# Splitting three of ten weight tiles with two GpSimd-queue loads instead of ScalarE and VectorE

## The chip, the cores and the metric

The kernel runs on one core of one Trainium2 chip. The metric is device time in microseconds (us) of one execution; a timed comparison gives the median of several runs of each kernel on the same chip. Engines are named as the profile names them: PE (TensorE matmul), PEld (TensorE weight load), DVE (VectorE), ACT (ScalarE), POOL (GpSimd), SP (SyncE, which here issues the loads).

## The reference

Two transformer-like blocks are run one after the other on 256 tokens of width 2048, all in float32. The first has a two-way gated recurrence, a short convolution, an output projection and a gated feed-forward; the second has a long convolution, an attention with forget gates, an attention over 256 memory rows and an output projection. The change touches the first block's feed-forward alone:

```python
D_FF = -(-8 * D_MODEL // (3 * 256)) * 256          # 5632
...
h2 = _rmsnorm(x, ffn_norm_w[l])
g, u = jnp.split(jnp.einsum('bsd,df->bsf', h2, w_gate_up[l]), 2, axis=-1)
x = x + jnp.einsum('bsf,fd->bsd', jax.nn.silu(g) * u, w_down[l])
```

## The kernel before, in words

*Products from parts.* TensorE multiplies float32 through the type F32R. To keep the precision, each operand is split in a high part (the value copied to F32R) and a low part (the value minus the high part), and a product is three matmuls: high x high, high x low, low x high (`tri`, lines 645 to 647; `proj`, lines 166 to 168). The activations are split once and kept in "units" (tiles of `upool`, eight buffers). The weights stream: `split` (L131) is `load` (L113: SP brings 256 rows x 512 columns, 512 KB, into a tile `raw`) followed by `parts_of` (L120: ACT copies `raw` to `wh`, then DVE subtracts `wl = raw - wh`). Since the helpers `act` (L63) and `tt` (L54) record every operation, ACT and DVE work stands under those two lines in the profile and is told apart by its tiles.

*Rings.* `raw_tile` (L108) takes the load tiles in turn: four of pool `wraw` outside the feed-forward, and during it `wraw` and `wraw2` (four each) alternately, so eight. The pairs `wh`, `wl` come from `wsp` (four) and, in the feed-forward, `wsx` (two), in a turn of six. A load can be issued only when the tile that it takes has been read for the last time.

*The feed-forward.* The 5632 hidden columns are worked in 11 pieces of 512 (index f). `hidden_pre(f)` (L649) computes gate and up products of one piece over eight steps p of 256 input rows each. In steps 0, 1, 3, 5, 7 the gate tile and the up tile are each split and multiplied plainly: two tiles of 12 products of 512 columns each, ten tiles a piece. In steps 2, 4, 6 a seven-product scheme is used (L685 to L711): DVE forms combinations `Ta` and `Tb` of the two loaded tiles, which are split too, and TensorE does 21 products. After p = 5 the bank X4 is read out and the hidden tile of the piece before is transposed there (`turn`, L733, line 739). At the end DVE and ACT combine the banks to the hidden tile `hd` (L713 to L730). All eight PSUM banks (five of `pmm`, three of `phd`) serve one piece.

*Parts.* The pieces are grouped in three parts (0 to 3, 4 to 7, 8 to 10; L748). After each part the down projection (`proj` with `w_down`, four column blocks) adds what its pieces contribute to the residual tile X (`residual`, two DVE additions a column block). The four units that hold the input of the feed-forward live through the whole stage; the units of a part's hidden tiles live until its down projection has read them.

*Order of the work.* The program is written in the order of the data; a scheduler with a timeline of its own orders the instructions on each engine, and `high_priority` (4000 for the splits) moves work ahead as far as its buffers allow. On each engine and queue the order is then fixed, and an instruction that waits holds those behind it.

Of the kernel before, what the change touches and what calls it, by code (L numbers as in the profile page):

```python
# [8 lines left out]
F32 = mybir.dt.float32  # L9
F32R = mybir.dt.float32r  # L10
# [3 lines left out]
ALU = mybir.AluOpType  # L14
# [6 lines left out]
CW = 512  # L21
# [8 lines left out]
def tile_two_blocks(  # L30
# [4 lines left out]
    nc = tc.nc  # L35
    x, mem, out = x[0], mem_2[0], out[0]
    w_in, w_out, w_gate_up, w_down = w_in[0], w_out[0], w_gate_up[0], w_down[0]
# [4 lines left out]
    wraw = ctx.enter_context(tc.tile_pool(name="wraw", bufs=4))  # L42
# [7 lines left out]
    def stt(out, in0, scalar, in1, op0, op1):  # L50
        nc.vector.scalar_tensor_tensor(out=out, in0=in0, scalar=scalar, in1=in1, op0=op0, op1=op1)  # L51

    def tt(out, a, b, op):
        nc.vector.tensor_tensor(out=out, in0=a, in1=b, op=op)  # L54
# [7 lines left out]
    def act(out, in_, func=AF.Copy, **kw):  # L62
        nc.scalar.activation(out=out, in_=in_, func=func, **kw)  # L63
# [4 lines left out]
    def bank(shape):  # L68
        return phd.tile(shape, F32, tag="h", name="h")
# [5 lines left out]
    def new_unit():  # L75
        return upool.tile([128, 4, 2, T], F32R, tag="u", name="u")
# [28 lines left out]
    more_raw = []  # L105
    more_w = []

    def raw_tile(nk, n):  # L108
        raw = (more_raw[-1] if more_raw else wraw).tile([128, nk, n], F32, tag="raw", name="raw")
        more_raw.reverse()  # L110
        return raw

    def load(w, r0, nk, c0, n):  # L113
        raw = raw_tile(nk, n)
        nc.sync.dma_start(
            out=raw, in_=w[r0:r0 + nk * 128, c0:c0 + n].rearrange("(k p) n -> p k n", p=128)
        )
        return raw

    def parts_of(raw, pool=None):  # L120
        if pool is None:
            pool = more_w[0] if more_w else wsp
            if more_w:
                more_w.append(more_w.pop(0))
        wh = pool.tile(list(raw.shape), F32R, tag="wh", name="wh")
        wl = pool.tile(list(raw.shape), F32R, tag="wl", name="wl")
        act(wh, raw)
        tt(wl, raw, wh.bitcast(F32), ALU.subtract)
        return wh, wl

    def split(w, r0, nk, c0, n, pool=None):  # L131
        with tc.high_priority(4000):
            return parts_of(load(w, r0, nk, c0, n), pool)

    def mm_bank():
        return pmm.tile([128, CW], F32, tag="p", name="p")
# [9 lines left out]
    def two(a):  # L146
        return a.rearrange("p (h b) -> p h b", h=2)
# [195 lines left out]
    with tc.tile_pool(name="rows", bufs=1) as rows:  # L343
        vb = rows.tile([nv, 128], F32, name="vb")
        for name, src, n in vectors:
            nc.gpsimd.dma_start(
                out=vb[off[name]:off[name] + n], in_=src.rearrange("(a b) -> a b", b=128)
# [26 lines left out]
    with tc.tile_pool(name="mk", bufs=1) as mkp:  # L374
# [11 lines left out]
        out=cums[:, :128], in_=cums[:, :128], pattern=[[1, 128]], compare_op=ALU.is_ge, fill=0.0,  # L386
# [5 lines left out]
        out=cmask, in_=cmask, pattern=[[-1, 128]], compare_op=ALU.is_ge, fill=NEG,  # L392
# [158 lines left out]
    for hf in range(2):  # L551
# [5 lines left out]
        for j in range(2):  # L557
# [4 lines left out]
            for a in range(2):  # L562
                k = 2 * j + a
                w = [cw3[:, 8 * i + 4 * hf + k:8 * i + 4 * hf + k + 1] for i in range(3)]
# [35 lines left out]
    ff = ExitStack()  # L600
    fp = ff.enter_context(tc.tile_pool(name="fp", bufs=1))
# [33 lines left out]

    more_raw.extend([wraw, ff.enter_context(tc.tile_pool(name="wraw2", bufs=4))])
    wsx = ff.enter_context(tc.tile_pool(name="wsx", bufs=2))
    more_w.extend([wsp, wsp, wsx, wsp, wsp, wsx])  # L640

    def tri(pt, left, right, st, sp):
        (xh, xl), (wh, wl) = left, right
        mh, ml = in_turn(wh), in_turn(wl)
        nc.tensor.matmul(pt, lhsT=xh, rhs=mh, start=st, stop=False)  # L645
        nc.tensor.matmul(pt, lhsT=xh, rhs=ml, start=False, stop=False)  # L646
        nc.tensor.matmul(pt, lhsT=xl, rhs=mh, start=False, stop=sp)  # L647

    def hidden_pre(f, between):  # L649

        five, three = [mm_bank() for i in range(5)], [bank([128, CW]) for i in range(3)]
        if f % 2:
            P2, P1, P4, P3, X4 = five
            P6, P7, P5 = three
        else:
            P1, P2, P6, P7, P5 = five
            P3, P4, X4 = three
        begun = set()

        def prod(pt, left, right, end=False):  # L660
            tri(pt, left, right, id(pt) not in begun, end)
            begun.add(id(pt))

        for p in range(8):
            u, a0 = x1u[p // 2], 2 * (p % 2)
            r0, end = 256 * p, p == 7

            def x_(a, t):
                sl = slice(t * 128, (t + 1) * 128)
                return u[:, a0 + a, 0, sl], u[:, a0 + a, 1, sl]  # L670

            if p not in sums7:
                for (b0, b1), c0 in (((P2, P4), f * CW), ((P3, X4), DFF + f * CW)):
                    wh, wl = split(w_gate_up, r0, 2, c0, CW)
                    for a in range(2):
                        for t, b in enumerate((b0, b1)):
                            prod(b, x_(a, t), (wh[:, a], wl[:, a]), a == 1 and (end or (b is X4 and p == 5)))
                if p == 5:
                    x4 = fp.tile([128, CW], F32, tag="x4", name="x4")
                    with tc.high_priority(4000):  # L680
                        act(x4, X4)
                    between(X4)
                    begun.discard(id(X4))
                continue
            F = sums7[p]  # L685
            with tc.high_priority(4000):
                g_ = load(w_gate_up, r0, 2, f * CW, CW)
                u_ = load(w_gate_up, r0, 2, DFF + f * CW, CW)
                B1 = parts_of(g_)
                Ta, Tb = (fp.tile([128, 2, CW], F32, tag=n, name=n) for n in ("Ta", "Tb"))  # L690
                tt(Ta[:, 0], u_[:, 0], g_[:, 0], ALU.subtract)
                tt(Ta[:, 1], u_[:, 1], u_[:, 0], ALU.subtract)
                W13 = parts_of(Ta)
                tt(Tb[:, 0], u_[:, 1], Ta[:, 0], ALU.subtract)
                tt(Tb[:, 1], g_[:, 1], Tb[:, 0], ALU.subtract)
                W24 = parts_of(Tb)
                B22 = parts_of(u_[:, 1:2])

            def at(w, a):
                return w[0][:, a], w[1][:, a]  # L700

            def form(i):
                return F[:, i, 0], F[:, i, 1]

            prod(P1, x_(0, 0), at(B1, 0), p == 6)
            prod(P2, x_(1, 0), at(B1, 1))
            prod(P5, form(0), at(W13, 0), p == 6)
            prod(P7, form(2), at(W13, 1), p == 6)
            prod(P6, form(1), at(W24, 0), p == 6)
            prod(P4, x_(1, 1), at(W24, 1))  # L710
            prod(P3, form(3), at(B22, 0))  # L711

        u2 = fp.tile([128, CW], F32, tag="u2", name="u2")  # L713
        u3 = fp.tile([128, CW], F32, tag="u3", name="u3")
        g = fp.tile([128, NT, CW], F32, tag="g", name="g")
        h = fp.tile([128, NT, CW], F32, tag="hd", name="hd")
        with tc.high_priority(4000):
            act(g[:, 0], P1)
            tt(u2, P6, g[:, 0], ALU.add)
            tt(u3, P7, u2, ALU.add)  # L720
            tt(g[:, 0], P2, g[:, 0], ALU.add)
            tt(x4, x4, u3, ALU.add)
            tt(g[:, 1], P4, u3, ALU.add)
            tt(x4, P5, x4, ALU.add)
            tt(u2, P5, u2, ALU.add)
            tt(x4, X4, x4, ALU.add)
            tt(u2, P3, u2, ALU.add)
        for t, up_ in enumerate((u2, x4)):
            act(g[:, t], g[:, t], AF.Silu, scale=rs1[:, t:t + 1])
            stt(two(h[:, t]), ordered(up_), rs1[:, t:t + 1], ordered(g[:, t]), ALU.mult, ALU.mult)  # L730
        return h
# [13 lines left out]

    st = new_stats()
    x2u = []
    for part in (range(0, 4), range(4, 8), range(8, 11)):  # L748
        gu = []
        waiting = lambda ps: None  # L750
        for f in part:
            h = hidden_pre(f, waiting)
            gu.append((new_unit(), f * CW))
            waiting = turn(h, gu[-1][0])
        waiting(bank([128, CW]))
        for c in range(4):
            residual(proj(gu, w_down, c * CW), c)
            if part[-1] == 10:
                x2u.append(unit_from(xk(c), lambda k, c=c: wfg[:, 4 * c + k:4 * c + k + 1]))
                stats_piece(st, xc(c), c)  # L760
# [290 lines left out]
    for u, r0 in out_units:  # L1051
        for k0 in (0, 2):
            pool = lw if len(parts) < 6 else wsp
            parts.append((u, k0, split(w_out2, r0 + k0 * 128, 2, 3 * CW, CW, pool)))
    for t in range(NT):
        sl = slice(t * 128, (t + 1) * 128)
        n = CW if t == 0 else CW // 2
        for c0 in range(0, CW, n):
            pt = mm_bank()[:, :n]
            cs = slice(c0, c0 + n)  # L1060
            for i, (u, k0, (wh, wl)) in enumerate(parts):
                for a in range(2):
                    k = k0 + a
# [7 lines left out]
            part = small.tile([128, 1], F32, tag="part", name="part")  # L1071
# [50 lines left out]
```

## Time and profile before

| | |
|---|---|
| three runs, median | 1612.77 us (1611.62 to 1613.57) |
| profiled execution | 1613.91 us |
| its span | 1611.9 us |
| mean granted TensorE clock | 0.998 |
| feed-forward stage, first to last start of L645 and after (in the span) | 523.4 to about 1166 us |
| loads from `w_gate_up` | 176 of 512.0 KB, 4.6 us in the median from issue to landing |

The profile describes one execution by its span; the execution's own time is longer by what lies around the span. A line of groups names line, engine, operation, tiles, count, busy time and mean, and behind the last bar the idle time of the engine just before them with what ended it. A row of waits names who waited for whom, the sum in us, how often, and the longest. A row of windows gives the busy time of each engine in a stretch with the number of instructions, then the granted clock, the DMA engines' busy share and GB/s. A row of the chain gives start, duration and what. A row of the DMA list gives count, size and the median time from issue to landing.

### The profile page before, as it was taken

How to read it: one execution, taken by the hardware profiler on the slowest of the kernel's cores; microseconds unless marked ns; L12 is line 12 of the kernel's file. 1: busy time of each engine (PE TensorE's matmuls, PEld its weight loads, DVE VectorE, ACT ScalarE, POOL GpSimd, SP SyncE). 2: the span in 40 equal slices, each digit the busy share in tenths (PEclk: the TensorE clock that was granted, in tenths of full speed). 3: DMA queues.
4: the chain of work that ended last, by engine and by line, in shares of the span. 5: the costliest groups of instructions: out<-in, count | busy, mean ns of one | idle time of the engine just before them, and what ended most of it. 6: DMA issues, size and time to landing. Idle time of an engine off the chain costs nothing.

```text
span 1611.9 us, 22433 instructions
## 1 busy us (share of the span) xinstructions
PE 1591.7 (99%) x8433; PEld 1411.7 (88%) x8433; DVE 1245.7 (77%) x1726; ACT 886.4 (55%) x1156; POOL 23.1 (1%) x57
## 2 busy tenths in 40 slices
PE   8999999999999999999999999999999999999998
PEld 7999999999988888888888888888889889998987
DVE  7769768765667899976699975799877999766754
ACT  4657557554545665543565554455546545555643
POOL 3000000000000000000000000000000000000000
PEclk9999999999999999999999999999999999999999
DMA  8765566466686666676666676666756567656564
GB/s 291 215 193 167 145 178 189 144 184 209 203 303 213 184 199 205 202 238 201 193 205 197 184 243 207 182 197 201 243 155 205 148 197 221 183 157 197 164 216 141
DMA packets 166892, 318.36 MB, mean 198 GB/s; under 512 B 12248, under 2 KB 13168, under 8 KB 166784
## 3 DMA queue, kind: packets, MB, share of 16 engines
q1 hardware_dynamic: 164304, 312.19, 62.8%
q10 hardware_dynamic: 2032, 4.60, 0.8%
q8 instruction: 66, 1.08, 0.3%
q14 instruction: 42, 0.34, 0.1%
q0 software_dynamic: 448, 0.14, 0.1%
HBM read 313.74 MB, written 3.15 MB: 197 GB/s over the span
## 4 chain that ended last, share of the span: by engine, by line
PE 77%; DVE 16%; issue 4%; DMA 3%; ACT 1%; ACTq 0%; DVEq 0%; POOLq 0%; POOL 0%
PE p L194 18%; PE p L167 11%; PE p L168 11%; PE p L166 11%; PE p L195 9%; DVE wl L54 8%; DMA raw<-in_w_gate_up_dram 2%; PE h L446 2%; PE p L646 2%; PE p L647 2%; PE p L645 2%; DVE Tb L54 1%; PE h L646 1%; PE h L647 1%; PE h L645 1%
## 5 line engine op out<-in xcount | busy, mean ns | idle before, releaser
L54 DVE TENSOR_TENSOR wl<-raw,wh 128x1024 fp32r<-128x1024 f32 (+1 forms) x580 | 685.0, 1193 | 269.0 <-ACT wh L63 265.8
L63 ACT ACTIVATE wh<-raw 128x1024 fp32r<-128x1024 f32 (+1 forms) x580 | 589.6, 1029 | 516.5 <-PE p L168 169.8
L194 PE MATMUL p<-u,wh 128*128 128x512 f32 x1392 | 458.7, 383 | 0.6 <-DVE sg L54 0.6
L195 PE MATMUL p<-u,wl 128*128 128x256 f32 x1392 | 365.6, 274 | 0.9 <-DVE wl L54 0.8
L167 PE MATMUL p<-wl,u 128*128 128x512 f32 x832 | 318.0, 383 | 0.9 <-DVE wl L54 0.9
L166 PE MATMUL p<-wh,u 128*128 128x512 f32 x832 | 313.3, 381 | 1.7 <-ACT u L63 1.2
L168 PE MATMUL p<-wh,u 128*128 128x512 f32 x832 | 313.6, 382 | 0.7 <-DVE u L51 0.7
L194 PEld LDWEIGHTS p<-u,wh 128*128 128x128 f32 x1392 | 260.1, 190 | 31.3 <-DVE sg L54 1.1
L195 PEld LDWEIGHTS p<-u,wl 128*128 128x128 f32 x1392 | 266.5, 191 | 8.3 <-DVE wl L54 1.6
L166 PEld LDWEIGHTS p<-wh,u 128*128 128x128 f32 x832 | 157.2, 189 | 24.1 <-ACT u L63 2.0
L167 PEld LDWEIGHTS p<-wl,u 128*128 128x128 f32 x832 | 157.5, 189 | 22.7 <-DVE wl L54 1.3
L168 PEld LDWEIGHTS p<-wh,u 128*128 128x128 f32 x832 | 157.0, 190 | 22.1 <-DVE u L51 1.3
L646 PE MATMUL p<-wl,u 128*128 128x512 f32 x341 | 130.1, 383 | 2.3 <-DVE wl L54 2.3
L647 PE MATMUL p<-wh,u 128*128 128x512 f32 x341 | 128.3, 379 | 0.0
L645 PE MATMUL p<-wh,u 128*128 128x512 f32 x341 | 123.7, 380 | 0.0
L646 PE MATMUL h<-wl,u 128*128 128x512 f32 x198 | 75.4, 381 | 2.0 <-DVE wl L54 2.0
L646 PEld LDWEIGHTS p<-wl,u 128*128 128x128 f32 x341 | 64.4, 189 | 14.3 <-DVE wl L54 5.6
L647 PE MATMUL h<-wh,u 128*128 128x512 f32 x198 | 75.1, 379 | 0.0
L645 PE MATMUL h<-wh,u 128*128 128x512 f32 x198 | 74.6, 382 | 0.3 <-DVE u L54 0.2
L645 PEld LDWEIGHTS p<-wh,u 128*128 128x128 f32 x341 | 64.5, 189 | 9.0
L647 PEld LDWEIGHTS p<-wh,u 128*128 128x128 f32 x341 | 64.5, 189 | 8.7
L54 DVE TENSOR_TENSOR Ta<-raw 128x512 f32<-128x512 f32 x66 | 42.8, 694 | 29.7 <-DMA raw<-in_w_gate_up_dram 29.5
(313 smaller groups left out, 1705.4 us busy)
## 6 DMA issues: line engine op xcount, KB each, us to landing
raw<-in_w_in_dram SPq DMA_DIRECT2D x232, 512.0 KB, 4.0
raw<-in_w_gate_up_dram SPq DMA_DIRECT2D x176, 512.0 KB, 4.6
raw<-in_w_down_dram SPq DMA_DIRECT2D x88, 512.0 KB, 4.9
raw<-in_w_out_dram SPq DMA_DIRECT2D x64, 512.0 KB, 4.8
raw<-in_w_mem_kv_dram SPq DMA_DIRECT2D x14, 512.0 KB, 6.1
xp<-in_x_dram SPq DMA_DIRECT2D x4, 512.0 KB, 7.1
X<-in_x_dram SPq DMA_DIRECT2D x4, 512.0 KB, 7.3
mp<-in_mem_dram SPq DMA_DIRECT2D x3, 512.0 KB, 7.6
```

The lines of the kernel that those rows point to most:

```text
L54: nc.vector.tensor_tensor(out=out, in0=a, in1=b, op=op)
L63: nc.scalar.activation(out=out, in_=in_, func=func, **kw)
L166: nc.tensor.matmul(pt[t], lhsT=u[:, k, 0, sl], rhs=mh, start=st, stop=False)
L167: nc.tensor.matmul(pt[t], lhsT=u[:, k, 0, sl], rhs=ml, start=False, stop=False)
L168: nc.tensor.matmul(pt[t], lhsT=u[:, k, 1, sl], rhs=mh, start=False, stop=sp)
L194: nc.tensor.matmul(pt[f], lhsT=wh[:, a, fs], rhs=both, start=st, stop=False)
L195: nc.tensor.matmul(pt[f][:, :T], lhsT=wl[:, a, fs], rhs=high, start=False, stop=False)
L446: nc.tensor.matmul(ps[:, h], lhsT=k[:, h, s * 128:(s + 1) * 128], rhs=q[:, h, t * 128:(t + 1) * 128], start=True, stop=True,)
L645: nc.tensor.matmul(pt, lhsT=xh, rhs=mh, start=st, stop=False)
L646: nc.tensor.matmul(pt, lhsT=xh, rhs=ml, start=False, stop=False)
L647: nc.tensor.matmul(pt, lhsT=xl, rhs=mh, start=False, stop=sp)
```

## The change

For p = 1, 3 and 5 the gate tile is no longer loaded and split by SP, ACT and DVE. A tile of 2048 columns takes both parts. A load on the GpSimd queue with a change of type writes the high part straight from the weights; ACT writes its negative to the low part; a second GpSimd-queue load adds the same weights to the low part. For p = 1 and 5 the tile is a new one, `fl`, with one buffer; for p = 3 it is a unit of `upool`. The load tiles become six (`wraw` four, `wraw2` two, in the turn wraw, wraw, wraw2). The pieces are grouped in four parts: 0 to 2, 3 to 5, 6 to 8, 9 and 10.

```diff
     def raw_tile(nk, n):
-        raw = (more_raw[-1] if more_raw else wraw).tile([128, nk, n], F32, tag="raw", name="raw")
-        more_raw.reverse()
-        return raw
+        pool = more_raw[0] if more_raw else wraw
+        if more_raw:
+            more_raw.append(more_raw.pop(0))
+        return pool.tile([128, nk, n], F32, tag="raw", name="raw")
...
+    def split_in_flight(pair, w, r0, c0):
+
+        wh, wl = pair
+        src = w[r0:r0 + 256, c0:c0 + CW].rearrange("(k p) n -> p k n", p=128)
+        with tc.high_priority(6000):
+            nc.gpsimd.dma_start(out=wh, in_=src)
+            act(wl, wh.bitcast(F32), scale=-1.0)
+            nc.gpsimd.dma_start(out=wl, in_=src, accum_op=ALU.add)
+        return wh, wl
...
-    more_raw.extend([wraw, ff.enter_context(tc.tile_pool(name="wraw2", bufs=4))])
+    wraw2 = ff.enter_context(tc.tile_pool(name="wraw2", bufs=2))
+    more_raw.extend([wraw, wraw, wraw2, wraw, wraw, wraw2])
...
-                    wh, wl = split(w_gate_up, r0, 2, c0, CW)
+                    if p in (1, 3, 5) and b0 is P2:
+                        if p == 3:
+                            unit = new_unit().rearrange("p a b t -> p (a b t)")
+                        else:
+                            unit = fp.tile([128, 2048], F32R, tag="fl", name="fl")
+                        halves_ = (unit[:, i * 1024:(i + 1) * 1024] for i in range(2))
+                        pair = [x.rearrange("p (k n) -> p k n", k=2) for x in halves_]
+                        wh, wl = split_in_flight(pair, w_gate_up, r0, c0)
+                    else:
+                        wh, wl = split(w_gate_up, r0, 2, c0, CW)
...
-    for part in (range(0, 4), range(4, 8), range(8, 11)):
+    for part in (range(0, 3), range(3, 6), range(6, 9), range(9, 11)):
```

## The prediction, made before the changed kernel was built

> **What bounds the kernel now.** I read the page first, then busy time by stage, then the waits of the gated feed-forward stage, then its chain.
>
> ```profile
> span 1611.9 us, 22433 instructions
> PE 1591.7 (99%) x8433; PEld 1411.7 (88%) x8433; DVE 1245.7 (77%) x1726; ACT 886.4 (55%) x1156; POOL 23.1 (1%) x57
> PE 77%; DVE 16%; issue 4%; DMA 3%; ACT 1%; ACTq 0%; DVEq 0%; POOLq 0%; POOL 0%
> ```
>
> TensorE is the bound, but 16% of the chain lies on VectorE. The change touches only the feed-forward stage (523 to 1166 us). By stretches, one gate-up piece (one f) each, except 698:773, which is a down projection, and 1141:1166, the last part's turn to it:
>
> ```profile
> core 0: us, PE busy (x) PEld busy (x) DVE busy (x) ACT busy (x) POOL busy (x), PEclk, DMA share, GB/s
> 698.00:773.00 75.00, 75.00 (x353) 65.66 (x352) 45.47 (x45) 32.23 (x32) 0.00 (x0) 1.00 0.70 213
> 814.50:856.00 41.50, 41.50 (x193) 35.65 (x192) 37.91 (x46) 23.12 (x26) 0.00 (x0) 1.00 0.64 204
> 856.00:897.50 41.50, 39.84 (x186) 33.84 (x185) 37.91 (x47) 24.16 (x28) 0.00 (x0) 1.00 0.61 190
> 1062.00:1103.00 41.00, 41.00 (x194) 35.91 (x193) 37.45 (x46) 23.18 (x27) 0.00 (x0) 1.00 0.64 204
> 1141.00:1166.00 25.00, 25.00 (x124) 21.84 (x122) 19.65 (x22) 11.72 (x13) 0.00 (x0) 1.00 0.77 239
> ```
>
> DVE is busy 37.9 of 41.5 us in a gate-up piece and 45.5 of 75 in a down projection; ACT has 17 us to spare per piece, POOL all of it. What TensorE can do at best comes from its starts: two rows of the timeline in an unbroken run of 33 products, and four transposes before the next product.
>
> ```profile
> 689.52 0.60 PE L739 MATMUL p<-ident,hd 128*128 128x128 f32 x4
> 689.87 0.46 PE L168 MATMUL p<-wh,u 128*128 128x512 f32 x1
> 690.17 0.38 PE L166 MATMUL p<-wh,u 128*128 128x512 f32 x1
> 697.29 0.38 PE L646 MATMUL p<-wl,u 128*128 128x512 f32 x1
> ```
>
> 7.12 us / 33 = 0.216 us a product, whatever the 0.38 us written beside it. A piece has five plain p of 24 products and three seven-product p of 21, so 183, and 8 transposes at 0.35/4: 183 x 0.216 + 0.7 = 40.2 us. The chain shows what it takes once it has fallen behind, and the groups of VectorE in that piece show why:
>
> ```profile
> 842.23 4.58 DMA raw<-in_w_gate_up_dram
> 850.56 1.14 DVE wl L54
> 855.17 1.13 DVE wl L54
> 883.77 4.54 DMA raw<-in_w_gate_up_dram
> 892.07 1.14 DVE wl L54
> L54 DVE TENSOR_TENSOR wl<-raw,wh 128x1024 fp32r<-128x1024 f32 x13 | 15.9, 1233 | 0.0
> L54 DVE TENSOR_TENSOR Ta<-raw 128x512 f32<-128x512 f32 x6 | 3.9, 704 | 3.6 <-DMA raw<-in_w_gate_up_dram 3.6
> ```
>
> The same subtraction stands at 850.56 and 892.07: 41.5 us a piece, 1.3 over TensorE's 40.2. DVE's loop fills them: 37.9 of work and one 3.6 us wait at Ta for a load that could be issued only when a load tile came free. Over the stage, TensorE's loss is
>
> ```profile
> DVE Ta L54 <- DMA raw<-in_w_gate_up_dram: 27.7, 10, 3.6
> PEld p L646 <- DVE wl L54: 5.6, 10, 1.2
> PEld h L646 <- DVE wl L54: 3.7, 5, 1.2
> PEld h L645 <- DVE u L54: 1.8, 4, 0.6
> ```
>
> 5.6 + 3.7 = **9.3 us** of weight loads held up by wl (the 1.8 us for u is the turned hidden tile, which the change leaves). This is all that there is to win here: 0.6%.
>
> **The change part by part.** Of the ten plain tiles of each piece three (p = 1, 3, 5, gate half) lose their SP load, ACT copy and DVE subtraction. A POOL cast load writes wh, ACT writes minus wh to wl, a POOL adding load puts the weights on top. Over 11 pieces: 33 SP loads and 33 subtractions go, 66 POOL loads come, ACT keeps its count.
>
> *DVE.* 3 x 1.13 = 3.4 us less a piece: 41.5 - 3.4 = 38.1, under TensorE's 40.2 with the Ta wait still in it. So the wl waits go: **-9.3**. Of the 1.3 us a piece only the part beyond TensorE's pace was ever lost, so more is not to be had; I keep **+1.0** for waits that come from the order of DVE's work, not its sum. What is late next is ACT (23 to 24 us a piece) and then nothing.
>
> *Four parts for three.* One more turn to a down projection and four more pairs of residual additions (8 x 0.69 = 5.5 us of DVE, by the Ta rows' size; beside 29.5 us of its idle time in a down projection: nothing on the path). No wait of lines 166 to 168 stands in the rows after the turns: +0.3. The last part has two pieces, so while the last hidden tile is finished only one unit's 24 products per column block are ready, 5.2 us less cover a block; the next block's products can stand in (five banks). Between 0 and 5.2 I take +1.0, as 1141:1166 shows TensorE full in that place. Shorter parts also give DVE its pause sooner; that is inside the 9.3.
>
> *Six load tiles for eight.* A piece now issues 13 SP loads, so the ring spans 6/13 of a piece (18.6 us) where it spanned 8/16 (20.1). In order, the tile of p = 2's second half now waits for p = 7's first instead of p = 6's, but four to five subtractions then lie before Ta. I take 0; the other end is a second 3.6 us wait, 38.1 + 3.6 = 41.7, 1.5 over TensorE, for the five pieces that are third or later: 6 to 8 us.
>
> *The chain of the two POOL loads* decides. One tile, fl, serves p = 1 and p = 5. Its next cast can start only when TensorE has read it. From the end of p = 1's gate products to p = 5: 12 + 21 + 24 + 21 = 78 products, **16.8 us**; from p = 5's to the next p = 1: 12 + 21 + 24 + 24 = 81 and 8 transposes, **18.2 us**. (p = 3 has a unit of its own and a whole piece.) In that time: cast, negation, addition. The trace has no such load of this size, so by the nearest rows:
>
> ```profile
> raw<-in_w_gate_up_dram SPq DMA_DIRECT2D x176, 512.0 KB, 4.6
> mp<-in_mem_dram SPq DMA_DIRECT2D x1, 128.0 KB, 2.8
> mp<-in_mem_dram ACTq DMA_DIRECT2D x1, 128.0 KB, 4.7
> vm<-in_mem_norm_g_dram ACTq DMA_DIRECT2D x1, 8.0 KB, 2.2
> vb<-in_mem_norm_g_dram POOLq DMA_DIRECT2D x1, 8.0 KB, 4.9
> vb<-in_lb_bwd_dram POOLq DMA_DIRECT2D x1, 4.0 KB, 6.2
> v<-in_conv_w_dram POOLq DMA_DIRECT2D x1, 62.0 KB, 5.2
> L63 ACT ACTIVATE wh<-raw 128x1024 fp32r<-128x1024 f32 x13 | 13.3, 1054 | 5.5 <-PE h L647 3.7 <-PE p L647 1.8
> 10.42 0.54 POOL L352 DMA_DIRECT2D v<-in_conv_w_dram  x1
> ```
>
> Low end: both as SP's, 4.6 + 1.05 + 4.6 = 10.3. High end: POOL's surcharge 6.2 - 2.2 = 4.0 on each, and the addition moves its 512 KB twice (another 4.6 - 2.2 = 2.4): 8.6 + 1.05 + 1.5 behind other ACT work + 11.0 = 22.2. In the crowded start two like 128 KB loads already differ by 1.9, so of POOL's 2.7 (4.9 - 2.2) I count about 1.7: cast 6.3, negation 1.05 + 0.5, addition 6.3 + 1.2 = 7.5, in all **15.4**. It fits by 1.4 us; loads spread, so I put +1.5 for the pieces where it doesn't. The six issues a piece, 6 x 0.54 = 3.2 us, lie on an idle POOL; behind a waiting addition stands only the next cast, whose tile is still being read. ACT waits in order at each negation, wh copies behind it, for two or three us at most if it comes early; it has 17 us a piece.
>
> By the Trainium skill (DMA: Bandwidth & Descriptors, section Anatomy of one DMA) a load issued from GpSimd takes about 2.0 us and its bytes at 436 GB/s, an estimate of 3.2 us here, with which the chain would be 3.2 + 1.6 + 3.2 = 8.0 and the +1.5 would drop out: 1605.8. The trace's 4.9 us for 8 KB says the fixed part is longer in the start of this kernel.
>
> *Sum:* -9.3 + 1.0 + 0.3 + 1.0 + 0 + 1.5 = -5.5. The profiled execution took 1613.9 us (its span and 2.0 around it), 1.1 over the median 1612.8 of the three runs; against the median that is **1607.3**. A change under 0.2% (3.2 us) can't be told from none.
>
> **The rivals.** (a) *Slower: the two loads don't fit.* With a chain of C us each p = 5 waits C - 16.8 (11 times) and each p = 1 within a part C - 18.2 (7 times). The other terms give -7.0, so it breaks even at C = 17.4 and is slower by more than 0.2% from 17.7. At 19: 24 + 6 - 7 = +23, 1636. At 22.2: 59 + 28 - 7 = +80, 1693. For it: one buffer, two loads in series, an addition nobody has timed here; against it: SP's loads land in 4.6 and the order of products can be arranged around a late pair. (b) *No change.* C between 16.9 and 17.7, or the second Ta wait of 6 to 8 us, or the last turn's 5.2: each gives the 9.3 back, 1610 to 1615. (c) *The transfers become the bound.* DMA share is 0.61 to 0.64 in a piece with 16 loads; 13 + 3 casts + 3 additions at double weight make 22, 0.88. From an addition costing 3.0 loads' worth the share passes 1 by (16 + 9)/16 x 0.64; at 4 it is 1.12, 45 us a piece, +53: about 1660. The Trainium skill (the same page, section Issuing engines are not separate DMA queues) speaks for it: loads of all queues run on the same 16 engines, so POOL's queue adds no bandwidth. No run here shows POOL loads beside a full SP stream.
>
> **How the numbers follow.** Forecast, gain kept: 0.52 (1603 to 1609.5 as its own range; 1603.5 is all 9.3 won). No change: 0.18. Two loads too slow: 0.24. Transfers: 0.06. So faster 0.52, same 0.18, slower 0.30. The range starts a little below 1603.5 and reaches into (a) as far as a chain of 19: 1602 to 1636.
>
> **What would show it.** Right: PEld waits on wl in the stage fall from 9.3 to about 1 us, DVE is busy about 34.5 us a piece, and the bare starts of pieces lie 40 to 40.6 apart. The chain: fl's cast lands about 6.3 after issue, its addition about 7.5. Wrong: TensorE waits at L645 or L646 for a DMA or an ACT write of fl (rival a), SP's 4.6 us grows past 7 with a DMA share near 1 (c), or a DVE wait at Ta above 3.6 (b).

## The result, and the profile after

The changed kernel is slower: 1627.62 us in the median of four runs (1625.04 to 1630.81) beside 1613.17 for the kernel before, a ratio of 1.0094 [1.0080, 1.0108], so 0.8 to 1.1% where 0.3% of gain was forecast. The time lies inside the range given, on the wrong side of no change. The profiled execution took 1630.81 us, 3.2 over its median, so the rows below overstate the loss by about a sixth. A run more than 1.5% above the fastest of its kernel counts as slow and stays out of medians and ratios; that is one run below, of the kernel with the negation on GpSimd.

In the new kernel `tri`'s products are L657 to L659, `proj`'s L177 to L179, the casting load is L137, the adding load L139. From the page: the span, the engines, the chain's shares by engine, and the two queues that carry weights (q1 is SP's, q0 GpSimd's; packets, MB, share of 16 engines' span).

```profile
span 1629.1 us, 22469 instructions
PE 1596.4 (98%) x8433; PEld 1413.2 (87%) x8433; DVE 1212.4 (74%) x1701; ACT 880.0 (54%) x1156; POOL 86.9 (5%) x123
PE 74%; DMA 9%; DVE 7%; issue 7%; ACT 2%; POOL 0%; ACTq 0%; POOLq 0%; DVEq 0%
q1 hardware_dynamic: 155328, 294.88, 57.1%
q0 software_dynamic: 18400, 34.75, 10.3%
```

The feed-forward stage as one stretch, from its first product to the first product of the next block, of the kernel before and then of the changed one:

```profile
core 0: us, PE busy (x) PEld busy (x) DVE busy (x) ACT busy (x) POOL busy (x), PEclk, DMA share, GB/s
523.00:1208.00 685.00, 680.00 (x3192) 590.19 (x3191) 565.23 (x660) 369.12 (x415) 1.36 (x4) 1.00 0.65 202
```

```profile
523.00:1225.00 702.00, 685.92 (x3190) 592.12 (x3189) 536.25 (x640) 363.76 (x415) 62.74 (x66) 1.00 0.76 220
```

The whole loss lies here: 702 us for 685, with what follows equally long in both (403 to 404 us). VectorE was relieved as planned, by 565.2 - 536.3 = 29.0 us. What became of it stands in the changed kernel's waits in the stage (who, for whom, us, times, longest):

```profile
DVE wl L54 <- ACT wh L63: 97.0, 66, 6.2
DVE Ta L54 <- DMA raw<-in_w_gate_up_dram: 57.1, 11, 7.9
ACT fl L63 <- DMA fl<-in_w_gate_up_dram: 33.4, 18, 8.8
PEld p L658 <- DVE wl L54: 6.8, 7, 1.9
PEld h L657 <- ACT wh L63: 6.1, 4, 3.0
PEld p L657 <- ACT wh L63: 3.9, 2, 3.5
PEld p L658 <- DMA fl<-in_w_gate_up_dram: 0.4, 1, 0.4
```

VectorE's wait at Ta grew to 57.1 us from 29.5 in the kernel before (27.7 of them after 523 us), by about as much as VectorE was relieved. TensorE waited for the pair `fl` itself only 0.4 us; it waits, as before, for VectorE's wl, and now 10.0 us for ScalarE's wh, where that was 0.8. The page's DMA list (KB each, median us from issue to landing):

```profile
raw<-in_w_gate_up_dram SPq DMA_DIRECT2D x143, 512.0 KB, 4.9
fl<-in_w_gate_up_dram POOLq DMA_DIRECT2D x44, 512.0 KB, 5.9
u<-in_w_gate_up_dram POOLq DMA_DIRECT2D x22, 512.0 KB, 8.4
```

One loss can be followed from end to end in the chain (start, duration, what; fl is p = 5's and p = 1's tile, u here p = 3's):

```profile
597.27 7.47 DMA fl<-in_w_gate_up_dram
...
604.83 1.07 ACT fl L63
...
606.18 1.19 POOL fl L139
607.37 0.76 POOL u L137
608.13 8.88 issue
...
617.06 0.72 POOL u L139
617.77 9.23 DMA fl<-in_w_gate_up_dram
...
628.07 1.05 ACT wh L63
```

GpSimd's queue works through cast, add, cast, add in order. At 608 to 617 it stands at the adding load for u, whose negation sits on ScalarE behind an operation that waits 4.9 us for VectorE; the cast for fl is queued behind it, is issued at 617.77 and takes 9.23 us; ScalarE waits 8.77 us in order for its negation, with wh copies behind. VectorE's wl then waits 6.18 us for wh, and TensorE stops for 2.7 us, until 629.16. In the kernel before, the same stretch of the chain was VectorE at work and the loads that it waits for at Ta.

From 610 to 625 us the DMA engines were full: three loads of SP, then the adding load for u and the cast for fl beside them (columns as above; a share of about 1 means that the times of the packets fill all 16 engines):

```profile
614.00:617.00 3.00, 3.00 (x17) 2.63 (x17) 3.00 (x6) 1.95 (x3) 0.00 (x0) 1.00 1.05 391
619.00:621.00 2.00, 1.96 (x9) 1.61 (x9) 2.00 (x5) 0.00 (x0) 0.00 (x0) 1.00 1.09 242
```

Then comes a cost of its own, in four windows of 1 us of the changed kernel (columns as above):

```profile
628.00:629.00 1.00, 0.00 (x0) 0.00 (x0) 0.00 (x0) 1.00 (x2) 0.54 (x1) 1.00 0.00 0
629.00:630.00 1.00, 0.84 (x3) 0.49 (x3) 0.86 (x1) 1.00 (x3) 0.66 (x1) 1.00 0.00 0
631.00:632.00 1.00, 1.00 (x4) 0.82 (x3) 1.00 (x2) 1.00 (x3) 0.00 (x0) 0.50 0.94 145
634.00:635.00 1.00, 1.00 (x7) 0.87 (x6) 1.00 (x2) 0.00 (x0) 0.00 (x0) 1.00 0.94 360
```

And its products, from the timeline:

```profile
631.40 0.63 PE L659 MATMUL h<-wh,u 128*128 128x512 f32 x1
631.83 0.63 PE L657 MATMUL h<-u 128*128 128x512 f32 x1
632.26 0.63 PE L658 MATMUL h<-u 128*128 128x512 f32 x1
```

After the stop the granted clock is 0.50 for 3.4 us, and products start 0.43 us apart in place of 0.216. This happens twice in the stage (630.3 and 1009.2) and never in this stage of the kernel before. Note also the DMA share of 0.00 from 628 to 630: while all wait, the engines that move data have nothing to do, though they were full until 625.

### The profile page after: what moved, and what is told of

It reads as the page before. It is cut to its first block, busy times and chain, and to the rows that moved or that the text cites. A ratio compares the mean times of both kernels' runs of the same rounds, so it can differ in the third digit from the quotient of the medians.

```text
span 1629.1 us, 22469 instructions
## 1 busy us (share of the span) xinstructions
PE 1596.4 (98%) x8433; PEld 1413.2 (87%) x8433; DVE 1212.4 (74%) x1701; ACT 880.0 (54%) x1156; POOL 86.9 (5%) x123
## 3 DMA queue, kind: packets, MB, share of 16 engines
q1 hardware_dynamic: 155328, 294.88, 57.1%
q0 software_dynamic: 18400, 34.75, 10.3%
## 4 chain that ended last, share of the span: by engine, by line
PE 74%; DMA 9%; DVE 7%; issue 7%; ACT 2%; POOL 0%; ACTq 0%; POOLq 0%; DVEq 0%
PE p L205 18%; PE p L178 10%; PE p L179 9%; PE p L177 9%; PE p L206 9%; DMA fl<-in_w_gate_up_dram 6%; DVE wl L54 3%; PE p L658 2%; PE p L659 2%; PE p L657 2%; PE h L457 2%; DMA raw<-in_w_gate_up_dram 2%; PE h L657 2%; PE h L659 1%; PE h L658 1%
## 5 line engine op out<-in xcount | busy, mean ns | idle before, releaser
L54 DVE TENSOR_TENSOR wl<-raw,wh 128x1024 fp32r<-128x1024 f32 (+1 forms) x547 | 642.0, 1185 | 273.6 <-ACT wh L63 271.7
L63 ACT ACTIVATE wh<-raw 128x1024 fp32r<-128x1024 f32 (+1 forms) x547 | 552.8, 1025 | 461.9 <-PE p L179 138.9
L178 PE MATMUL p<-wl,u 128*128 128x512 f32 x832 | 317.7, 383 | 3.6 <-DVE wl L54 3.5
L177 PE MATMUL p<-wh,u 128*128 128x512 f32 x832 | 311.3, 382 | 2.6 <-DVE g L54 1.7
L179 PE MATMUL p<-wh,u 128*128 128x512 f32 x832 | 311.1, 382 | 2.0 <-DVE u L51 2.0
L178 PEld LDWEIGHTS p<-wl,u 128*128 128x128 f32 x832 | 157.3, 189 | 27.4 <-DVE wl L54 6.6
L177 PEld LDWEIGHTS p<-wh,u 128*128 128x128 f32 x832 | 157.1, 189 | 25.7 <-DVE g L54 2.1
L179 PEld LDWEIGHTS p<-wh,u 128*128 128x128 f32 x832 | 156.5, 189 | 23.2 <-DVE u L51 2.8
L658 PE MATMUL p<-wl,u 128*128 128x512 f32 x245 | 94.1, 384 | 4.2 <-DVE wl L54 4.2
L657 PE MATMUL p<-wh,u 128*128 128x512 f32 x245 | 92.7, 380 | 3.1 <-ACT wh L63 3.1
L659 PE MATMUL p<-wh,u 128*128 128x512 f32 x245 | 92.8, 379 | 0.0
L54 DVE TENSOR_TENSOR Ta<-raw 128x512 f32<-128x512 f32 x66 | 42.4, 682 | 57.2 <-DMA raw<-in_w_gate_up_dram 57.1
L657 PE MATMUL h<-wh,u 128*128 128x512 f32 x162 | 62.8, 391 | 4.6 <-ACT wh L63 4.5
L658 PE MATMUL h<-wl,u 128*128 128x512 f32 x162 | 62.0, 383 | 0.4 <-DVE wl L54 0.4
L659 PE MATMUL h<-wh,u 128*128 128x512 f32 x162 | 61.9, 382 | 0.0
L658 PEld LDWEIGHTS p<-wl,u 128*128 128x128 f32 x245 | 46.3, 189 | 12.8 <-DVE wl L54 6.7
L657 PEld LDWEIGHTS p<-wh,u 128*128 128x128 f32 x245 | 46.3, 189 | 10.5 <-ACT wh L63 3.5
L659 PEld LDWEIGHTS p<-wh,u 128*128 128x128 f32 x245 | 46.4, 189 | 6.2
```

Source lines behind the costliest of these rows:

```text
L177: nc.tensor.matmul(pt[t], lhsT=u[:, k, 0, sl], rhs=mh, start=st, stop=False)
L178: nc.tensor.matmul(pt[t], lhsT=u[:, k, 0, sl], rhs=ml, start=False, stop=False)
L179: nc.tensor.matmul(pt[t], lhsT=u[:, k, 1, sl], rhs=mh, start=False, stop=sp)
```

## The experiments

Each was timed against the kernel before on its own chip. Three readings stood against each other: the ring or the new parts are to blame; ScalarE's in-order wait for the casting load is; or the GpSimd loads slow the SP loads that VectorE waits for.

**Parts alone.** The kernel before with

```diff
-    for part in (range(0, 4), range(4, 8), range(8, 11)):
+    for part in (range(0, 3), range(3, 6), range(6, 9), range(9, 11)):
```

> The kernel before with nothing changed but four parts (3, 3, 3, 2 pieces). Theory A (ScalarE waits in order at each negation for a GpSimd load and holds its weight copies): four parts are not the cause, 1608 to 1614 us, since the third piece of each part still pays and the fourth is gone. Rival D (the extra turn to a down projection costs): about +4 us, 1617, with TensorE waits at lines 166 to 168 after the turns as at 841 to 853 us of the changed kernel.

1608.55 us, 0.9978 [0.9969, 0.9988]: faster, by 0.1 to 0.3%. Its waits in the stage:

```profile
DVE Ta L54 <- DMA raw<-in_w_gate_up_dram: 22.8, 11, 3.7
PEld p L646 <- DVE wl L54: 2.4, 6, 0.9
PEld h L646 <- DVE wl L54: 1.3, 2, 1.0
```

The 9.3 us of held weight loads fall to 3.7 with no tile moved. In the kernel before, 6.1 of the 9.3 us stand in the third piece after a pause (a down projection, in which VectorE gets ahead) and 1.6 in the fourth. With parts of three there is no fourth, and the third pieces wait 2.7 us.

**Parts and ring.** The same, and the six load tiles of the change:

> The kernel before with four parts and the ring of six load tiles, no GpSimd weight load: the changed kernel without its in-flight tiles. Theory A: within 3 us of the run with four parts alone. Rival C (the six-tile ring): all 16 loads of a piece go through six tiles, so at least the whole +14.5 us, 1627 or more, with the wait of VectorE at Ta for its load well above 27.7 us.

1610.14 us, 0.9992 [0.9982, 1.0001], with a Ta wait of 14.3 us, shorter than with eight tiles. Against the parts alone the ring costs about 2 us, and the intervals overlap. TensorE's held weight loads on wl are 1.4 us here, with all ten tiles still split by VectorE. All else that was lost comes with the split in flight.

**What the relief is worth.** The changed kernel, with the three tiles neither loaded nor split; a resident tile is multiplied in their place:

```diff
-                        unit = ...
+                        unit = x1u[0].rearrange("p a b t -> p (a b t)")
-                        wh, wl = split_in_flight(pair, w_gate_up, r0, c0)
+                        wh, wl = pair
```

> The changed kernel in which the three tiles are neither loaded nor split: TensorE multiplies by a resident tile instead, so these three tiles of each piece are left out of the result. Four parts, six load tiles, 13 loads a piece. It is the relief alone, without GpSimd loads, negations and their waits. By all theories 1603 to 1608 us: the 9.3 us of waits on wl go. If it stays at 1610 or above, the relief of VectorE was never worth what the prediction said.

1608.44 us, 0.9971 [0.9961, 0.9981], just above what was expected. With the three tiles free of charge the kernel is not measurably faster than with the four parts alone. Two waits, in the stage:

```profile
DVE Ta L54 <- DMA raw<-in_w_gate_up_dram: 40.5, 11, 5.0
PEld p L658 <- DVE wl L54: 0.6, 1, 0.6
```

TensorE hardly waits for wl. The stage is 2.4 us shorter than with parts and ring (676.5 for 678.9; before 684.8), 3.4 us by the ratios, so this is about all that splitting elsewhere can bring beside them. What follows the stage took 407.9 us in the profiled execution where it takes 403.4 in the kernel before: TensorE stopped twice for 1.2 us, until 1212.46 and 1214.67, and then ran at half clock for 3.4 us. A Ta wait of 40.5 us does little harm here: VectorE is still early enough for TensorE. It shows something else: with the tiles gone VectorE waits 4.4 to 4.9 us at Ta in the second and third pieces of a part, without any GpSimd load. The loads and negations of the split cost 1.0094/0.9971, so 1.2% or 20 us, against this kernel.

**Without p = 3.** Is it p = 3's adding load, ahead of fl's cast on the queue?

```diff
-                    if p in (1, 3, 5) and b0 is P2:
+                    if p in (1, 5) and b0 is P2:
```

> The changed kernel with p = 3 split in the old way, so only p = 1 and 5 (tile fl) come by the GpSimd queue. Theory A with its sharper form (the p = 3 load pair stands on the GpSimd queue ahead of fl's cast, which then lands after 8 to 9 us while ScalarE waits): ScalarE's longest wait for fl falls from 8.8 to below 4 us, the 2 us stops of TensorE in the third piece go, 1612 to 1618. Rival B (all queues share the DMA engines, extra traffic): a third of the loss goes, about 1623. Rival C (ring): 1627 or more, as 14 loads a piece go through six tiles.

1623.6 us, 1.0071 [1.0052, 1.0090]. The longest wait of ScalarE for fl fell from 8.8 to 4.2 us, and only a quarter of the loss went, as the reading by traffic had it: the one that blamed p = 3's addition missed. Its chain shows the other way to lose:

```profile
971.45 2.96 DVE wl L54 x3
974.41 0.02 issue
974.42 7.74 DMA raw<-in_w_gate_up_dram
...
982.28 0.79 DVE Ta L54 x2
...
985.36 0.48 PE p L658
```

VectorE's last subtraction frees a load tile at 974.4, SP's load into it takes 7.74 us (the like one in the chain before took 4.54), VectorE stands still for all of it, and TensorE stops for 3.1 us, until 985.36. No GpSimd tile is in this chain. A GpSimd load is beside it, though: a cast for fl, issued at 972.3, and an SP load, issued at 973.3, were under way too, and all three landed between 980.7 and 982.2. The windows of that load (the DMA share stands last but one):

```profile
974.40:976.00 1.60, 1.60 (x9) 1.39 (x9) 0.00 (x0) 1.36 (x2) 0.00 (x0) 1.00 0.93 292
976.00:978.00 2.00, 2.00 (x11) 1.76 (x10) 0.00 (x0) 1.62 (x3) 0.00 (x0) 1.00 0.98 282
978.00:980.00 2.00, 2.00 (x13) 1.77 (x12) 0.00 (x0) 0.00 (x0) 0.00 (x0) 1.00 0.67 247
980.00:982.20 2.20, 2.20 (x12) 1.74 (x10) 0.00 (x0) 1.36 (x2) 0.00 (x0) 1.00 0.05 20
```

The engines were full for the first 3.6 us. In the kernel before, the like load met shares of 0.92 and 0.83 in its first 3.6 us, and was through a good 3 us sooner.

**The negation on GpSimd**, so that ScalarE waits for no load:

```diff
-            act(wl, wh.bitcast(F32), scale=-1.0)
+            nc.gpsimd.tensor_scalar(out=wl, in0=wh.bitcast(F32), scalar1=-1.0, scalar2=None, op0=ALU.mult)
```

> The changed kernel with the negation on GpSimd in place of ScalarE, so that no ScalarE instruction waits for a GpSimd load. Theory A: the waits of ScalarE for fl (41 us in all) and the stops of TensorE on wh in the third pieces go, 1612 to 1618; the chain of the two loads gets 1 to 3 us longer and may show as a wait of TensorE for fl. Rivals B and C: no change, 1625 to 1630.

1642.0 us in the median of three runs (1629.24 to 1652.52), 1.0183 [1.0117, 1.0248]: far off what was expected. The negation takes 3.3 us there in the median in place of 1.05, up to 12.2, and now TensorE waits for the pair itself:

```profile
PEld p L658 <- DMA fl<-in_w_gate_up_dram: 33.3, 13, 7.2
```

It says nothing on ScalarE's wait, since it brought a wait of its own; it shows how little room the chain has.

**Two casting loads.** No negation, and the second load casts into wl instead of adding (the traffic stays, ScalarE is out of it):

```diff
-            act(wl, wh.bitcast(F32), scale=-1.0)
-            nc.gpsimd.dma_start(out=wl, in_=src, accum_op=ALU.add)
+            nc.gpsimd.dma_start(out=wl, in_=src)
```

> The changed kernel without the negation and with a second casting load in place of the adding one: the same bytes by the GpSimd queue, no ScalarE instruction that waits for them (the low parts are wrong, so part of the computation is changed). Theory A (ScalarE's wait in order is the main cause): 1605 to 1612. Rival B (traffic on the shared DMA engines makes the exposed loads of VectorE late): 1616 to 1626, with VectorE's wait at Ta still above 45 us.

1619.41 us, 1.0038 [1.0023, 1.0053]: inside what the reading by traffic gave, outside the other's. The wait at Ta is 54.2 us. With no engine between the loads, the kernel is still slower than before.

**No adding load**: the casting load and the negation stay, the line with `accum_op` goes.

> The changed kernel without the adding load (the weights are left out of the low part): half of the GpSimd traffic, the negation and its wait kept. Theory A: nearly all of the loss stays, 1620 or more. Rival B: about half of it goes, 1613 to 1618.

1618.05 us, 1.0030 [1.0018, 1.0042], at the upper edge of what the reading by traffic gave. ScalarE waited 25.9 us for fl's cast in it, and yet most of the loss was gone. It moves as many bytes as the kernel before (318.36 MB in both), so more traffic is not what it loses by. Its loss against parts and ring (a stage of 686.6 us for 678.9) stands in the first piece: TensorE stops for 2.0 us until 528.98 and for 3.3 until 540.39, and a spell of half clock adds some 2.6. The GpSimd queue's totals, to be held against the page of the changed kernel:

```profile
q0 software_dynamic: 9424, 17.44, 3.7%
```

The casts take 3.7% of the DMA engines' time; the adding loads, counted with the same bytes, 10.3 - 3.7 = 6.6%, so 1.8 times as much. The 66 casts of the run before this one took 7.1%, twice the 33.

**The negation without the wait.** All 66 loads as in the change; ScalarE negates a resident tile, so that it waits for no load:

```diff
-            act(wl, wh.bitcast(F32), scale=-1.0)
+            act(wl, x1u[0]...[:, :1024]..., scale=-1.0)
```

> The changed kernel with the negation reading a resident tile instead of the cast one: same loads, same adding load, same ScalarE work, but ScalarE waits for no load (the low parts are wrong, so part of the computation is changed). If ScalarE's wait for the cast makes the 8 us between the changed kernel and the run with two casting loads: 1617 to 1621. If the adding load's own cost does: 1624 or more.

1627.38 us, 1.0089 [1.0075, 1.0102], the same as the change. The waits:

```profile
DVE Ta L54 <- DMA raw<-in_w_gate_up_dram: 69.9, 15, 9.3
PEld p L658 <- DVE wl L54: 11.7, 7, 4.4
PEld h L658 <- DVE wl L54: 4.8, 2, 3.6
```

ScalarE's wait for fl is gone and the loss is not: it moved to Ta and wl.

**One tile of three**, p = 1's:

```diff
-                    if p in (1, 3, 5) and b0 is P2:
+                    if p == 1 and b0 is P2:
```

> The changed kernel with p = 1 alone in flight, so the tile fl is used once a piece and has about 38 us from one use to the next instead of 16.8 and 18.2. Four parts, six load tiles. If the tight reuse is what makes the cast land late and ScalarE wait: within 3 us of the run with ring and parts alone, 1608 to 1613. If it is the traffic alone, two of four GpSimd loads for fl remain of the run with p = 1 and 5: half of its loss over the ring-and-parts run, 1615 to 1618.

1616.88 us, 1.0027 [1.0017, 1.0038]. With 22 loads and fl used once a piece there is no tight reuse, and it still costs 0.35% over parts and ring (1.0027/0.9992), as the reading by traffic had it. Only the number agrees: its SP loads were hardly later with a GpSimd load beside them (4.9 us in the median for 4.65), so what it loses by is not shown.

**p = 3's alone**, with the eight load tiles of the kernel before and four parts:

> The changed kernel with p = 3 alone in flight (a unit with 38 us between its uses, no tile fl) and the eight load tiles of before: a third of the traffic, one negation a piece. Both theories: 1607 to 1613. Below 1608.5 us it would be the best version so far; a stop of TensorE at the start of the stage (5 us in the changed kernel, where two casts for p = 3 of the first pieces stand beside the load for Ta) should still be seen under rival B.

1610.66 us, 0.9986 [0.9976, 0.9995]: the mildest form, and still not better than the four parts alone. Of the stop at the start of the stage 1.5 us are left, until 536.5.

**Not in the first piece** (f = 0 is split as before):

```diff
-                    if p in (1, 3, 5) and b0 is P2:
+                    if f and p in (1, 3, 5) and b0 is P2:
```

> The changed kernel with the first piece split in the old way, so no GpSimd load lies in the turn from the output projection to the first piece. If the 5.2 us of TensorE stops at 528 and 539 us come from the two casts for p = 3 there: 1621 to 1624; if they come from the six load tiles or the first piece itself: 1626 or more.

1622.13 us, 1.0057 [1.0043, 1.0071], some 6 us less by the ratios, as expected; of these 1.5 us would go by the three tiles fewer alone, as an eleventh of the 16 us that the split costs against parts and ring. In the changed kernel two casts for u are issued at 508 and 513 us, before the stage, and SP's load behind them is late:

```profile
514.36 1.24 DVE wl L54
515.61 7.58 DMA raw<-in_w_gate_up_dram
...
523.28 0.76 DVE Ta L54 x2
```

From there TensorE stops for 1.7 us at 528.1 and, on the wh row of 3.9 us quoted above, for 3.3 us at 539.5. The DMA share is 1.11 from 517 to 519, and 0.85 in the run without the first piece. There one of the two casts is left, the one at 508; the like load took 4.08 us, Ta started at 520.03, both stops were gone, and TensorE stopped for 0.8 us at 537.6.

**Five parts**, the kernel before with parts of 3, 2, 2, 2 and 2 pieces:

> The kernel before with five parts (3, 2, 2, 2, 2 pieces), eight load tiles, nothing in flight. If the waits on wl come only from the third piece of a part on, since VectorE's lead from a down projection lasts about two pieces, four of the last waits go and the extra turn costs below 1 us: 1605.5 to 1608, below the run with four parts. If turns cost 2 us or more each: 1609 or above.

1608.44 us, 0.9974 [0.9964, 0.9983]: the same as four parts and just above what was expected. What VectorE gains in the pieces it gives back in the turns: the held weight loads on wl fall from 3.7 to 2.2 us in the gate-up products and rise from 0.4 to 1.5 in the down projections. These two are the best versions found, 3.5 to 4.2 us under the kernel before.

## Why the prediction was wrong

The loads can be put in a ladder, each against the kernel before on its own chip:

| kernel | ratio | step |
|---|---|---|
| three tiles free | 0.9971 | |
| + 33 casts (and ScalarE waiting for them) | 1.0030 | +9.5 us |
| 33 more casts, no negation | 1.0038 | +1.3 us, not told from 0 |
| adding loads in place of these, negation without a wait | 1.0089 | +8 us |
| ScalarE's wait for the cast (the change) | 1.0094 | +0.8 us, not told from 0 |

The waits of VectorE at Ta that exceed 4 us, behind the first piece, sum to 32.6 us with the tiles free, 31.5 with the 33 casts, 40.9 with 66, 54.0 with the resident negation, and 46.1 in the changed kernel. So the first step of the ladder isn't made there: it is the first piece, as said above. From 33 casts to 66 these waits grow by 9 us and the time hardly, as ScalarE waits for no cast there. The adding loads' step goes with them. In the changed kernel ScalarE's wait takes the place of some of them, and the time is the same.

*The step that failed* is the cost of the GpSimd loads: +1.5 us, for their fit into the time of one tile, and nothing for whoever shares the DMA engines with them. They cost 16 us against parts and ring (1.0094/0.9992), 20 against the tiles for free. In the sum the error sits in "38.1, under TensorE's 40.2 with the Ta wait still in it", which kept that wait at 3.6 us. VectorE's work did fall to 33 to 34.5 us a piece, but its wait at Ta was 6.0 to 7.9 us in the second and third pieces of the parts, so that its loop came back to TensorE's 40.2 us and above. Two things made the wait longer:

- The load behind Ta lost its cover, the work that VectorE still has while the load is under way. In the kernel before, SP issued it 1.1 to 2.6 us before VectorE ran out of work. In the changed kernel, with three subtractions fewer in a piece, SP issued it for seven of eleven waits only when VectorE had nothing left, so its whole latency is idle time; with the tiles free that is 4.4 to 4.9 us. The prediction's "four to five subtractions then lie before Ta" did not hold: there was none.
- The load itself landed later beside the GpSimd loads: after 5.8 to 7.7 us in these seven, where it took 4.2 to 4.8 with the tiles free. Over the stage, an SP load issued while a GpSimd load was under way landed after 5.95 us in the median (99 loads, 90th percentile 7.8), another after 4.75 (82); in the kernel with the resident negation after 7.1 and 4.5.

*DVE.* The relief was right in size: 33 x 1.13 less 5.5 for the residual's additions is 31.8 us, and 29.0 were measured. But it is not what TensorE was short of: 2.4 us of stage time at best beside parts and ring. The 9.3 us of wl waits were there to be won; the four parts, which I costed at +1.3 and whose gain I put inside the 9.3, took more than half of them by themselves, and with the ring all but 1.4 were gone, without a further gain in time.

*The ring* at 0: right within about 2 us, and a second Ta wait in a piece did not come from it. (Its other end was priced for five pieces that are third or later; the new parts have three.) By itself it did not uncover the load behind Ta, which has 1.7 to 4.1 us of cover with parts and ring.

*The chain* of 15.4 us: right. From cast to landed addition the trace has 11.1 to 16.6 us for 20 of the 22 uses of fl, and 20.2 and 21.8 for the first two, in the first piece; the shortest cast took 4.0 us, the median one for fl 5.9 (6.3 predicted), the addition 5.9 (7.5). The Trainium skill's estimate of 3.2 us (DMA: Bandwidth & Descriptors, Anatomy of one DMA) is under every one of them: the trace decides for the longer. The pair was in time, so rival (a) did not happen here; it is what the negation on GpSimd, with 33.3 us of waits for fl, made of it.

*ACT's wait*, "two or three us at most", reached 8.8 us. I overlooked that p = 3's pair, though in a tile of its own, shares GpSimd's queue with fl: its addition, waiting for ScalarE, held fl's cast, and ScalarE then waited for that cast. Taking this wait away alone gained nothing that can be measured, because what it covered came to light: the wait at Ta grew from 57.1 to 69.9 us.

*Rival (c)* named the right resource, and looked at it by the average. That stayed at 0.76 and was not the bound. But in stretches of 2 us the share was 0.9 or more for 40% of the stage (523 to 1160 us), and for 18% in the kernel before; the slow loads above were under way in such stretches. So the DMA engines were full in bursts, and TensorE paid where a burst held a load without cover. It cost about a third of (c)'s 53 us. *Rival (b)*'s sign, a Ta wait above 3.6 us, came true at 7.9, with another cause and at about twice its price.

*The sum* also lacked the first piece: about 5 of the 14.5 us are two stops at the start of the stage, from casts issued ahead of it. It lacked the clock too, with about 3 us (below).

Still open: how ScalarE's waits and the slower loads divide the loss, as each covers the other; and why an adding load disturbs the others so much more than a second cast, beyond its 1.8-fold time on the engines. GpSimd loads issued only in the down projections, or later in the first piece, were not tried, nor was a plain load more on SP's queue, which would tell the traffic from the queue that brings it.

## What to carry to other kernels

Before a load moves to another queue, look for loads whose landing is already somebody's idle time, and price what one more stream does to their latency; a mean DMA share of 0.65 says nothing on it, so look at the share while that very load is under way. Taking work off an engine can also uncover such a load, since the work was its cover. Ask when in a stage the waits begin, not only how long they are: here most came in the third piece after a pause, and a pause more often was worth as much as splitting three plain tiles of ten elsewhere for free (3.5 us against 3.4, by the ratios). An operation that goes load, engine, load ties two in-order queues together, and each can then hold the other's unrelated work.

## What the runs showed of the hardware

The clock: in the changed kernel stops of TensorE of 2.1 and 2.7 us were each followed by 3.4 us at a granted clock of 0.50. In the kernel with the tiles free two stops of 1.2 us within 3.5 us were. Spells of 6.8 us stood in the stage of the kernel without additions and of three others. By start times all this cost 3 us in the changed kernel, 5 in the one with the resident negation, none in the stage before the change. It is no plain threshold: the 3.3 us stop until 539.5 in the changed kernel was followed by none. The Trainium skill (TensorE: Matmul & The Clock Gate, What's actually happening) has the clock halved after an idle window of about 3.4 us that runs free of the kernel; the spell's length here, 3.413 us, agrees with the window, but the stops that led to it were shorter than one.

The DMA engines: 33 adding loads took 6.6% of the engines' time where 33 casts of the same size took 3.7%. In the changed kernel the engines, with a share of 1.05 and 1.09, moved 391 GB/s from 614 to 617 us, with no addition under way, and 242 from 619 to 623, with one.

GpSimd as an engine: its negation of 128 x 1024 took 3.3 us in the median and up to 12.2, beside ScalarE's 1.05. And its issues: a cast took 0.7 to 1.2 us of its time and an addition 1.2, where 0.54 of a small load had been the price. GpSimd was busy for 62.7 of the stage's 702 us, so these issues themselves held nothing up.
